# Moving loads, two block transpositions and four totals within the heads stage of a two-layer hybrid backbone kernel

## Chip, cores and metric
One core of a Trainium2 chip. The metric is the device time of one execution in microseconds, the median of several runs.

## The reference, cut to what matters
The reference is a two-layer network on 1024 latent and 256 context tokens, width 1024, all in float32. Layer 0 is a bidirectional gated DeltaNet with 4 heads (beside a pooling branch), layer 1 a short convolution; each layer ends in a mixture of 16 experts. The change touches DeltaNet and the modulation only:

```python
gam = jnp.cumsum(log_decay.reshape(b, h, n, c), axis=-1)
diff = gam[..., :, None] - gam[..., None, :]
decay = jnp.where(incl, jnp.exp(jnp.where(incl, diff, 0.0)), 0.0)
kk = jnp.einsum('bhnid,bhnjd->bhnij', k, k)
t_mat = jnp.eye(c) + jnp.where(strict, kk * decay, 0.0) * beta[..., :, None]
u  = solve(t_mat, v * beta[..., None])        # unit lower triangular
wk = solve(t_mat, k * (beta * jnp.exp(gam))[..., None])
...
sh1, sc1, g1, sh2, sc2, g2 = jnp.split(silu(c) @ ada_w[i] + ada_b[i], 6, axis=-1)
```

For each head, direction and chunk a triangular matrix is made from the decays and from k k^T, and inverted. The modulation is a product of one row with a 1024 x 6144 matrix for each layer.

## The kernel before, in words
The program is one long list of steps that a planner puts in order. The planner places, on each engine, what is ready first, and among ready work what was traced first (`urgent` moves steps ahead by an offset). So the trace order is a preference, the data and buffers decide, and each engine, and SP's queue of DMA issues too, then runs its list strictly in order.

The heads stage is the loop over H = 4 heads in `hybrid_dit_kernel` (L1632 to L1648). `weave` (L832) mixes several lists of steps in proportion: step i of a list of n stands at (i + 0.5)/n. In turn h of the loop three weaves follow one another: the last projection span of head h with `front(h, 0)`; the first span of head h + 1 with `front(h, 1)`, the first eight steps of `invert(h - 1)` and the first half of the modulation's steps; the second span of head h + 1 with `front(h, 2)` and `base(h)`, the other eight steps of `invert(h - 1)`, the decays of head h + 1, and the second half of the modulation's steps.

What the lists hold:
- `project` (L1068): matmuls (tile pq, through `mm3`, L140 to L142), six to a product step, and `convolve` on ScalarE and VectorE (L1090, L1091).
- `decays` (L1140): three groups of chunks (4, 4 and 2). A step allocates the tile L (tag L4 with 4 buffers, two heads' worth; tag L2 with 2), loads the rows of decays from memory, broadcast over the partitions (L1149, two DMAs), and subtracts and masks them on VectorE (L1155, 16 operations of 128x128 for the two large groups, 4 for the small). A last step takes the exponential (L1162).
- `front` (L1166): norms, transposes to token order, k k^T and q k^T (pkk), VectorE's products with L (L1223, L1228), stores of the corner blocks (L1236).
- `base` (L1247): loads the 32x32 corner blocks of 40 items in two directions into X and M (L1262), turns the 40 x 1024 block of X into M (L1264, always on VectorE), clears X (L1265, L1266), eliminates 31 columns with two operations each (L1275, L1278; on GpSimd for heads 0 to 2, on VectorE for head 3), turns the 104 x 1024 result (L1282, always on VectorE) and stores it (L1287).
- `invert` (L1301): loads W (L1313) and builds the 128x128 inverses from the blocks with small matmuls (pinv, L1332) in 16 steps: load, then pairs up to `fourth`, then `fifth` and `sixth` for each of three groups. `fifth` reads L for the last time; after it L's buffer is free for the load of the head after next. `sixth` ends in VectorE's copies into Y (L1392, L1393).
- `ada_blocks` (L782): 2048 columns of the modulation's row, in `parts` of 512 columns (4 parts in the heads stage, 1 elsewhere): eight `products` (DMA of `ada_w`, L797, into a ring of three buffers; VectorE adds into the one buffer adsum, L800 and L802), then `total` (a TensorE matmul with ones, L810, into pad).

The four lines that set the counts before:

```python
        steps += [lambda h=h, k=k: products(h, k) for k in range(KD)] + [lambda h=h: total(h)]   # 9 a part
                weave(project(h + 1, 0), front(h, 1), before[:8], ada[h][:18])
                weave(
                    project(h + 1, 1), base[:-3], before[8:] + mx.decays(h + 1, E[h + 1], heads), ada[h][18:],
```

After the loop come the remaining projections (pz), `base(3)` on VectorE, two scans of two heads each (psc; the second needs sets of all inverses, loaded from memory), and the rest of the network.

## Time and profile before

| what | us |
|---|---|
| median of 3 runs | 1884.71 |
| the runs | 1881.73 to 1886.57 |
| the profiled execution | 1886.57 |
| its span, first to last instruction | 1884.9 |
| TensorE busy in the span | 1659.9 (88%) |
| VectorE busy | 1302.0 (69%) |
| ScalarE busy | 899.6 (48%) |
| GpSimd busy | 531.3 (28%) |

The heads stage lies between 136 and 453 us of the span. Engines are PE (TensorE, its weight loads PEld), DVE (VectorE), ACT (ScalarE), POOL (GpSimd) and SP, whose queue issues the DMAs. In a timeline the bracket at the end of a row is the time that the engine stood idle before it, and what ended that. The clock is the mean granted clock of TensorE, 1.00 for 2.4 GHz.

### The profile page before, as it was taken

The page shows a single profiled execution, that of the slowest core. Times are in us where ns is not written, and L with a number is a line of the kernel's source. Part 1 is how long each engine was busy: PE and PEld are TensorE (multiplying, and loading weights), DVE is VectorE, ACT ScalarE, POOL GpSimd, SP SyncE. Part 2 cuts the span into 40 slices and gives each one's busy share as a digit, 9 for nine tenths or more (in the row PEclk, how much of TensorE's full clock was granted, in tenths as well). Part 3 has the DMA queues.
Part 4 walks back from the last instruction along what each step waited for, and adds up shares of the span by engine and source line. Part 5 has one row for each costly group of instructions (what it writes and reads, how often), then busy time and mean ns, then how long its engine had stood idle before and what let it go on. Part 6 is the DMA issues. An engine that isn't in the chain of part 4 may idle for free.

```text
span 1884.9 us, 26146 instructions
## 1 busy us (share of the span) xinstructions
PE 1659.9 (88%) x9593; PEld 1332.0 (71%) x9593; DVE 1302.0 (69%) x1978; ACT 899.6 (48%) x1586; POOL 531.3 (28%) x551
## 2 busy tenths in 40 slices
PE   6999998789979881999999989999999559989995
PEld 2998875667867661777777777888887347767773
DVE  4628785657778876778888768343444658788897
ACT  3635332523742353777766452101133358778673
POOL 4310286471331154112121261000022512112222
PEclk7989998879999985999999999999999769999998
DMA  7417665649576965799999657422264449999995
GB/s 285 148 35 228 216 200 132 160 151 283 165 291 205 380 223 209 251 350 347 373 360 358 195 181 261 169 95 83 95 226 155 172 137 320 373 338 364 371 334 196
DMA packets 261399, 443.72 MB, mean 235 GB/s; under 512 B 46522, under 2 KB 108715, under 8 KB 257175
## 3 DMA queue, kind: packets, MB, share of 16 engines
q1 hardware_dynamic: 252198, 408.76, 62.7%
q0 software_dynamic: 9072, 33.30, 7.0%
q8 instruction: 75, 1.23, 0.3%
q14 instruction: 54, 0.43, 0.1%
HBM read 368.65 MB, written 73.35 MB: 234 GB/s over the span
## 4 chain that ended last, share of the span: by engine, by line
PE 49%; DVE 14%; DMA 7%; ACT 5%; issue 5%; SPq 2%; POOL 1%; DVEq 0%; ACTq 0%; POOLq 0%
PE py L466 5%; PE gu L141 5%; PE gu L142 4%; PE gu L140 4%; PE pin L140 4%; PE pin L141 4%; PE pin L142 4%; DVE wlo L89 3%; PE po L140 3%; PE po L141 3%; PE po L142 3%; ACT whi L88 2%; PE py L469 1%; DVE junk L315 1%; ACT oh L367 1%
## 5 line engine op out<-in xcount | busy, mean ns | idle before, releaser
L89 DVE TENSOR_TENSOR wlo<-raw,whi 128x2048 fp32r<-128x2048 f32 (+3 forms) x245 | 471.4, 1956 | 79.1 <-ACT whi L88 79.0
L88 ACT CAST whi<-raw 128x2048 fp32r<-128x2048 f32 (+3 forms) x271 | 420.7, 1597 | 219.7 <-PE pin L141 77.7
L141 PE MATMUL gu<-wlo,xh 128*128 128x512 f32 x512 | 209.4, 410 | 11.4 <-DVE wlo L89 11.4
L140 PE MATMUL gu<-whi,xh 128*128 128x512 f32 x512 | 206.7, 408 | 7.7 <-ACT whi L88 6.2
L142 PE MATMUL gu<-whi,xl 128*128 128x512 f32 x512 | 205.3, 404 | 0.4 <-DVE xl L135 0.4
L476 POOL DMA_INDIRECT acc<-y,idx x31 | 80.7, 2603 | 363.7 <-DVE y L471 346.2
L141 PE MATMUL pin<-h1T,whi 128*128 128x512 f32 x384 | 149.9, 392 | 0.0
L142 PE MATMUL pin<-h1T,wlo 128*128 128x512 f32 x384 | 149.4, 391 | 0.0
L140 PE MATMUL pin<-h1T,whi 128*128 128x512 f32 x384 | 148.6, 396 | 0.0
L89 POOL TENSOR_TENSOR wlo<-raw,whi 128x1024 fp32r<-128x1024 f32 (+2 forms) x26 | 80.5, 3117 | 177.4 <-ACT whi L88 166.8
L141 PEld LDWEIGHTS gu<-wlo,xh 128*128 128x128 f32 x512 | 99.0, 193 | 37.2 <-DVE wlo L89 14.9
L140 PEld LDWEIGHTS gu<-whi,xh 128*128 128x128 f32 x512 | 98.8, 193 | 33.4 <-ACT whi L88 8.5
L142 PEld LDWEIGHTS gu<-whi,xl 128*128 128x128 f32 x512 | 98.6, 193 | 22.9 <-DVE xl L135 0.9
L466 PE MATMUL py<-whi,hh 128*128 128x512 f32 x256 | 104.2, 410 | 8.5 <-ACT hh L134 8.4
L802 DVE SCALAR_TENSOR_TENSOR adsum<-raw,cs,adsum 128x512 f32<-128x512 f32 (+1 forms) x77 | 94.9, 1233 | 21.8 <-DMA raw<-in_ada_w_dram 21.2
L466 PE MATMUL py<-wlo,hh 128*128 128x512 f32 x256 | 103.7, 406 | 0.1
L373 POOL DMA_INDIRECT xg<-table,idx x32 | 51.2, 1600 | 176.3 <-ACT idx L371 137.1
L140 PE MATMUL pq<-hT,whi 128*128 128x512 f32 (+1 forms) x256 | 99.0, 387 | 2.1 <-DVE cv L1090 2.0
L367 ACT ACTIVATE oh<-places,aff 128x128 f16<-128x128 f16 x256 | 77.9, 394 | 45.3 <-DVE aff L356 45.3
L141 PE MATMUL pq<-hT,whi 128*128 128x512 f32 (+1 forms) x256 | 98.4, 385 | 0.0
L142 PE MATMUL pq<-hT,wlo 128*128 128x512 f32 (+1 forms) x256 | 98.2, 384 | 0.0
L141 PE MATMUL po<-wlo,mh 128*128 128x512 f32 x224 | 91.6, 409 | 4.9 <-DVE wlo L89 4.9
(393 smaller groups left out, 3733.9 us busy)
## 6 DMA issues: line engine op xcount, KB each, us to landing
raw<-in_w_gate_dram SPq DMA_DIRECT2D x64, 1024.0 KB
raw<-in_w_up_dram SPq DMA_DIRECT2D x64, 1024.0 KB
raw<-in_w_down_dram SPq DMA_DIRECT2D x64, 1024.0 KB
raw<-in_ada_w_dram SPq DMA_DIRECT2D x32, 1024.0 KB
raw<-in_ada_w_dram SPq DMA_DIRECT2D x64, 256.0 KB
raw<-in_sc_w_in_dram SPq DMA_DIRECT2D x12, 1024.0 KB
table<-h SPq DMA_DIRECT2D x16, 520.0 KB
raw<-in_ev_w_in_dram SPq DMA_DIRECT2D x16, 512.0 KB
```

The costliest lines, as they stand in the source:

```text
L88: nc.scalar.copy(hi[:, part], raw[:, part])
L89: (lo_engine or e).tensor_sub(lo[:, part], raw[:, part], hi[:, part])
L140: nc.tensor.matmul(out, lhs[0], rhs[0], start=start, stop=False)
L141: nc.tensor.matmul(out, lhs[0], rhs[1], start=False, stop=False)
L142: nc.tensor.matmul(out, lhs[1], rhs[0], start=False, stop=stop)
L315: nc.vector.tensor_scalar(junk, self.v, cand.bitcast(F32), 0.0, op0=ALU.is_ge, op1=ALU.add, accum_out=cnt)
L367: nc.scalar.activation(oh[:, t, :], co.places, AF.Sign, bias=self.before[:, t, e : e + 1])
L373: nc.gpsimd.indirect_dma_start(out=xg, out_offset=None, in_=self.table[:, :], in_offset=bass.IndirectOffsetOnAxis(ap=idx, axis=0))
L466: nc.tensor.matmul(py, hh[:, k, :], g[w][:, k, :], start=k == w == 0, stop=False)
L469: nc.tensor.matmul(py, hl[:, k, :], g[0][:, k, :], start=False, stop=k == 3)
L476: self.scattered = nc.gpsimd.indirect_dma_start(out=self.acc[:, :], out_offset=bass.IndirectOffsetOnAxis(ap=idx, axis=0), in_=y, in_offset ...
L802: nc.vector.scalar_tensor_tensor(st["sum"], raw, cs[:, k, 0:1], st["sum"], op0=ALU.mult, op1=ALU.add)
```

## The change
Three edits, in the heads stage only.
1. `ada_blocks` with more than one part puts an empty step ahead of each `total` and one behind it: 11 steps a part where there were 9, 45 with the end where there were 37. The first weave of a turn takes 22 of them (two parts, as before) and the second the rest.
2. `decays` gives two lists: three `load` steps (tile and DMAs) and the `prepare` steps with the exponential. In turn 0, which has no inversion, the loads stand ahead of the preparation. In the others the list of the second weave is: fourth, fourth, fifth, sixth, fifth, sixth, load, fifth, load, sixth, load, then three preparations and the exponential: 15 steps where there were 12.
3. The two turning copies in `base` run on the engine of the columns: GpSimd for heads 0 to 2, VectorE as before for head 3.

```diff
@@ ada_blocks
     for h in range(parts):
-        steps += [lambda h=h, k=k: products(h, k) for k in range(KD)] + [lambda h=h: total(h)]
+
+        gap = [lambda: None] if parts > 1 else []
+        steps += [lambda h=h, k=k: products(h, k) for k in range(KD)] + gap + [lambda h=h: total(h)] + gap
     return steps + [end]
@@ Mixer0.decays
-        def prepare(c0, n):
+        def load(c0, n):
             e = pool.tile([P, 2, n, P], F32, tag=f"L{n}", name=co.name("L"), bufs=4 if n == 4 else 2)
             E.append(e)
             for d in range(2):
...
+
+        def prepare(g):
+            e, (c0, n) = E[g], GROUPS[g]
             for d in range(2):
                 for c in range(n):
                     nc.vector.scalar_tensor_tensor(
...
-        return [lambda c0=c0, n=n: prepare(c0, n) for c0, n in GROUPS] + [exp]
+        return [lambda c0=c0, n=n: load(c0, n) for c0, n in GROUPS], [lambda g=g: prepare(g) for g in range(len(GROUPS))] + [exp]
@@ Mixer0.base, begin and end
-            nc.vector.tensor_copy(M[0:40], X[0:40].rearrange("p r c -> p c r"))
+            engine.tensor_copy(M[0:40], X[0:40].rearrange("p r c -> p c r"))
...
-            nc.vector.tensor_copy(XT[:R], X[:R].rearrange("p r c -> p c r"))
+            engine.tensor_copy(XT[:R], X[:R].rearrange("p r c -> p c r"))
@@ hybrid_dit_kernel
-        weave(project(0, 1), mx.decays(0, E[0], heads))
+        loads, rest = mx.decays(0, E[0], heads)
+        weave(project(0, 1), loads + rest)
...
-                weave(project(h + 1, 0), front(h, 1), before[:8], ada[h][:18])
+                weave(project(h + 1, 0), front(h, 1), before[:8], ada[h][:22])
                 ahead = fetch(h + 2)
-                weave(
-                    project(h + 1, 1), base[:-3], before[8:] + mx.decays(h + 1, E[h + 1], heads), ada[h][18:],
-                )
+
+                loads, rest = mx.decays(h + 1, E[h + 1], heads)
+                after = before[8:]
+                if after:
+                    n = len(after)
+                    after = after[: n - 2] + [loads[0], after[n - 2], loads[1], after[n - 1], loads[2]]
+                else:
+                    after = loads
+                weave(project(h + 1, 1), base[:-3], after + rest, ada[h][22:])
```

## Rows read from the trace of the kernel before
**Rows 1.** The windows of the heads stage and of the first scan: from and to in us, length, then for PE, PEld, DVE, ACT and POOL the busy us and the number of instructions, then the mean granted clock, the share of the DMA engines and GB/s.
```profile
136.00:265.00 129.00, 125.47 (x657) 101.59 (x657) 98.82 (x229) 50.10 (x101) 43.26 (x55) 1.00 0.69 211
300.00:326.00 26.00, 22.02 (x286) 15.81 (x284) 14.58 (x22) 6.05 (x12) 23.32 (x39) 0.87 0.28 89
326.00:343.00 17.00, 6.34 (x43) 5.52 (x39) 14.67 (x36) 6.81 (x14) 9.20 (x13) 0.65 0.57 177
390.00:414.00 24.00, 15.68 (x79) 12.96 (x77) 16.53 (x51) 7.71 (x18) 18.17 (x26) 0.62 0.53 159
```
**Rows 2.** Who waited for whom, of TensorE alone, 130 to 500 us: us in total, times, longest.
```profile
PE pinv L1332 <- DVE Y L1393: 11.4, 2, 7.0
PE pad L810 <- DVE adsum L802: 7.0, 2, 4.0
```
**Rows 3.** The same of VectorE, 136 to 505 us.
```profile
DVE L L1155 <- DMA L<-d_gT: 21.1, 5, 6.6
DVE base L1264 <- DMA base<-d_blk: 16.2, 4, 6.2
DVE adsum L800 <- PE pad L810: 7.4, 3, 5.9
```
**Rows 4.** The chain that ended last, from 425 us on: start, us, what.
```profile
425.12 0.26 POOL base L1278
...
428.40 5.04 DMA d_inv<-base
...
433.89 1.57 SPq L1313
...
451.58 1.16 PE psc L1429 x8
...
513.37 4.96 DMA sets<-d_A
```
**Rows 5.** Windows of 10 us around three stalls of TensorE, columns as in rows 1.
```profile
260.00:270.00 10.00, 6.94 (x34) 5.54 (x34) 10.00 (x21) 4.21 (x10) 9.06 (x13) 0.83 0.70 184
280.00:290.00 10.00, 8.41 (x36) 6.78 (x34) 4.19 (x11) 1.28 (x3) 3.91 (x7) 0.66 0.62 136
300.00:310.00 10.00, 6.02 (x174) 3.49 (x172) 5.62 (x9) 2.86 (x7) 8.74 (x17) 0.85 0.37 124
310.00:320.00 10.00, 10.00 (x62) 7.91 (x63) 3.65 (x6) 1.52 (x3) 9.13 (x16) 0.80 0.08 28
```
**Rows 6.** Timelines of VectorE and of TensorE around 282 us: start, us, engine, line, operation, what, idle before.
```profile
281.24 1.08 DVE L1282 COPY base<-base 104x1024 f32<-104x1024 f32 x1 [2.15 <-POOL base L1278]
...
283.82 0.79 PE L140 MATMUL pq<-hT,whi 128*128 128x512 f32 x1 [1.59 <-DVE cv L1090]
```
**Rows 7.** Timeline of TensorE: two totals, and two projection matmuls one behind the other at full clock.
```profile
264.68 1.04 PE L810 MATMUL pad<-adsum,ones 128*32 128x512 f32 x2 [3.06 <-DVE adsum L802]
...
299.32 0.39 PE L141 MATMUL pq<-hT,whi 128*128 128x512 f32 x1
299.55 0.40 PE L142 MATMUL pq<-hT,wlo 128*128 128x512 f32 x1
...
308.01 1.92 PE L810 MATMUL pad<-adsum,ones 128*32 128x512 f32 x2 [3.98 <-DVE adsum L802]
```
**Rows 8.** Timelines of VectorE and of SP's queue, 291 to 297 us.
```profile
291.40 0.49 DVE L800 TENSOR_SCALAR adsum<-raw,cs 128x512 f32<-128x512 f32 x1 [5.90 <-PE pad L810]
295.50 1.12 DVE L1264 COPY base<-base 40x1024 f32<-40x1024 f32 x1 [3.62 <-DMA base<-d_blk]
...
286.74 4.26 SPq L1313 DMA_DIRECT2D W<-d_inv  x4
...
293.41 1.43 SPq L797 DMA_DIRECT2D raw<-in_ada_w_dram  x3
```
**Rows 9.** Timelines of SP, TensorE and VectorE around the loads of the decays' rows, and VectorE's turning copy at 425 us.
```profile
143.07 2.91 SPq L1149 DMA_DIRECT2D L<-d_gT  x6
...
317.50 2.88 SPq L1149 DMA_DIRECT2D L<-d_gT  x4
...
316.77 1.15 PE L1332 MATMUL pinv<-W,L 64*64 64x64 f32 x32
...
311.69 1.33 DVE L1375 COPY Y<-W 64x512 f32<-64x512 f32 x2
...
320.68 2.90 DVE L1155 SCALAR_TENSOR_TENSOR L<-L,g_G,maskf 128x128 f32<-128x128 f32 x4 [6.62 <-DMA L<-d_gT]
...
425.53 1.10 DVE L1282 COPY base<-base 104x1024 f32<-104x1024 f32 x1
```
**Rows 10.** Groups by line of 130 to 500 us (busy us, mean ns of one, idle before), and two single column operations of GpSimd from its timeline.
```profile
L1265 POOL MEMSET base<- 128x1024 f32 x4 | 3.8, 956 | 32.0 <-DVE base L1264 22.0 <-DMA d_q<-cv 10.0
L1266 POOL TENSOR_SCALAR_AFFINE_SELECT base<-base 128x1024 f32<-128x1024 f32 x4 | 5.8, 1457 | 0.1
L1264 DVE COPY base<-base 40x1024 f32<-40x1024 f32 x4 | 4.4, 1108 | 16.2 <-DMA base<-d_blk 16.2
L1282 DVE COPY base<-base 104x1024 f32<-104x1024 f32 x4 | 4.3, 1068 | 2.2 <-POOL base L1278 2.2
...
320.49 0.65 POOL L1275 TENSOR_TENSOR base<-base,base 104x255 f32<-104x255 f32 x1
323.51 1.18 POOL L1275 TENSOR_TENSOR base<-base,base 104x255 f32<-104x255 f32 x1
```

## The prediction, made before the changed kernel ran
> **What bounds the kernel now.** First the windows by stage [rows 1]. The change works in the heads stage, 136 to 453 us. Up to 265 us TensorE is busy 125.5 of 129 us at full clock and sets the pace; from 265 to 414 us it loses time, in three of these stretches: busy 22.0 of 26, 6.3 of 17, 15.7 of 24, at a mean granted clock of 0.87, 0.65 and 0.62. So what this stage is worth is read from what TensorE waits for. Its own waits [rows 2] name two things: 11.4 us for the copies into Y (VectorE, L1393) and 7.0 us for the modulation's last product (VectorE, L802) ahead of a total (L810). Both name VectorE, though VectorE is not full there: VectorE's waits [rows 3] show that its queue stands still, 21.1 us for the decays' rows from memory, 16.2 us for the blocks ahead of their transposition (L1264), 7.4 us for a total; ahead of the second transposition (L1282) it waited 2.2 us for GpSimd [rows 10]. The three parts of the change aim at these four waits. What follows the stage starts from it: in the chain that ended last [rows 4] GpSimd's last column of head 2, the turned blocks' store and the load of W stand one behind the other up to the sets of the second scan. I therefore count a microsecond won before 414 us as won at the end, if this chain comes earlier too.
>
> **Each stall of TensorE costs twice.** Where it idles, the granted clock falls to the lower of its two levels (1.2 GHz) for some microseconds after. Slices of 10 us [rows 5]: a mean of 0.66 means that 6.8 us of the slice ran at 1.2 GHz, so 3.4 us are lost beside the idle time itself; 0.83 is 1.7 us lost, 0.85 and 0.80 behind one another are 3.5.
>
> **T1, transposition L1282 off VectorE.** At 281 us, at the end of head 0's base, VectorE waits 2.15 us for GpSimd, turns the blocks in 1.08, and only then does the convolution that TensorE wants: TensorE idles 1.59 us and goes on at the low clock [rows 6]. With the turning on GpSimd this wait has no reason left. 1.59 plus half of the 3.4 us at the low clock (part of the slice lies ahead of this stall's end, so I don't take it all): **3.3 us**, bounds 0 and 5.0. The same copy for heads 1 and 2 has no stall of TensorE right behind it: nothing more.
>
> **T2 and T3, totals a step later, and L1264 off VectorE.** TensorE stood twice at a total: 3.06 us at 262 and 3.98 at 304 us [rows 7]. A step put ahead of them is about one product step of the woven projection, six matmuls at 0.23 us from one start to the next [rows 7], 1.4 us: TensorE has that much to do while the last product ends. T3 (the stall at 262): 1.4 of 3.06 plus half of 1.7 of clock: **2.2**, bounds 0 and 4.8. T2 (the stall at 304): VectorE also comes earlier, by the copy L1264 itself, 1.1 us; its 3.62 us wait ahead of that [rows 8] I don't count, because the next data of the modulation were issued on SP's queue only at 293.41, behind the loads of W [rows 8]. So 1.1 and 1.4 of 3.98, plus half of 3.5: **4.2**, bounds 0 and 7.5. The step behind a total gives VectorE as much again before it overwrites the sum; the single buffer of the sum stays.
>
> **T4, loads of the decays' rows as steps.** The load is late because the buffers are: for head 2 it is issued at 317.50, 0.7 us after the matmuls that read the old tiles began at 316.77, on an SP queue that had nothing else [rows 9]. A step of its own cannot go ahead of those reads. What changes is that the weave has 15 steps where it had 12, so the third of them, the reading one, stands at 2.5/15 and not 2.5/12 of a stretch of 26 us (300 to 326 [rows 1]): 1.1 us earlier for the rows of heads 2 and 3 alike, **2.2 us**. Bounds: 0, and 11.4, the whole of TensorE's wait for Y, which stands behind VectorE's 6.62 us wait for the rows and the 16 operations on them [rows 9]. Head 1's rows were loaded from 143.07 on [rows 9], long before they are read, and cost nothing either way. The loads of each head are six issues on SP as before, and the queue stood at this wait before as well, so its wait costs nothing new.
>
> **T5, the last head.** It still uses VectorE for its columns, and L1282 of head 2 stands among the first of them (425.53, 1.10 us [rows 9]); gone from there the columns end earlier: **1.1 us**, bounds 0 and 1.1.
>
> **T6, what GpSimd pays.** No row shows such a copy on GpSimd. Bounds by the nearest rows [rows 10]: below, the memset of 128x1024, 0.96 us; a pass with one input over as much, affine_select, 1.46; above, the column operation, 0.65 us for 255 elements, so 2.6 for 1024, and 1.18 for 255 beside VectorE's work, so 4.7. The column operations read across the rows in steps, as the turning does, so I take 2.6, against 1.07 to 1.11 on VectorE [rows 10]: 1.5 us more. In heads 0 and 1 both copies are covered: GpSimd waited 22.0 us for L1264 in any case [rows 10], and between its last column and the next head's first copy it has nothing to do. In head 2 both lie on the chain of [rows 4]: **minus 3.0**, bounds plus 0.2 and minus 7.2. The Trainium skill (GPSIMD Engine Reference, Engine selection) says that passes with one input run at roughly VectorE's rate there: by that T6 would be 0 and the sum 10.3. Its section on performance pitfalls charges 2.9 cycles an element for reads in steps of over 8 bytes, here 128: an estimate of 2.5 us at its 1.2 GHz, and a sum of 7.5. No run here shows either.
>
> **What is late next.** T1 and T2 give TensorE 7.5 us by 317 us, but the reading matmuls at 316.77 also want Y's copies, which VectorE ended at 311.69 plus 1.33 [rows 9]: TensorE can come 3.7 us earlier, VectorE itself 1.1 more. I take 4.8 of the 7.5 and take off **2.7**.
>
> **Sum:** 3.3 + 2.2 + 4.2 + 2.2 + 1.1 - 3.0 - 2.7 = 7.3 us. The profiled execution took 1886.57 us (span 1884.9), 1.86 above the median of the runs, 1884.71. Against its own time that is 1879.3; against the median **1877.4 us**. A measurement of this kernel can tell about 0.3%, 5.7 us, from no change.
>
> **Rivals.**
> A, the wait for the rows goes too: earlier reads and lower priority of the 16 operations let Y's copies go first on VectorE. For it: they are separate steps now, and the loads and the operations had one place. Against: VectorE takes what is ready, and the operations were ready. 11.4 in place of T4's 2.2: 1868.2. 12%.
> B, VectorE's row of waits from 300 to 343 us takes back what TensorE wins: T1, T2 and T4 are lost in it, 2.2 + 1.1 - 3.0 = 0.3 is left: 1884.4. For it: VectorE does 14.7 of 17 us there with TensorE at 6.3 [rows 1]. 20%.
> C, slower: the totals come too late for VectorE. The sum has one buffer, so the next part's first product waits for the total; at 291.40 it had waited 5.90 us because TensorE had a row of matmuls ahead of the total [rows 8]. Put a step later, each of the 8 totals stands another 1.4 us behind; if VectorE gets to the next part before the second step has passed, that is 8 x 1.4 = 11.2 us of standing queue, and T2 and T3 are gone: 1884.71 - (3.3 + 2.2 + 1.1 - 3.0) + 11.2 = 1892.3. It decides where these waits, 7.4 us now, pass 15. Against: the step behind the total moves the product as well. 20%.
> D, the order on the engines stays what it was, since ready work goes first whatever step it was in, and the copies on GpSimd are covered: 1884.7. 6%.
> The forecast has 42%, with a range of its own from 1872 to 1882.
>
> **How the numbers follow.** Range 1866 to 1893: from A with a little of T4's clock up to C. Faster by over 0.3%, below 1879.1: A and 34 of the forecast's 42, 0.46. Within: the other 8, B and D, 0.34. Slower: C, 0.20.
>
> **What would show it.** T1: no wait of TensorE for a convolution at about 283 us, clock above 0.9 in that slice. T2 and T3: TensorE's wait for the modulation under 2 us in all (7.0 now). T4: VectorE's wait for the decays' rows still above 12 us, with the load still right behind the reading matmuls. T5: the last head's columns begin under 1 us after head 2's last column and run without a turning copy. T6: a turning copy on GpSimd of 2 to 3.3 us. I am wrong if the copy takes over 5 us, if VectorE's wait for totals grows, or if the first scan begins no earlier than at 451.58 us [rows 4].

## The result, and the profile after

| | before | changed |
|---|---|---|
| median | 1884.26 us (4 runs) | 1904.28 us (4 runs) |
| lowest to highest | 1881.73 to 1886.57 | 1898.26 to 1907.00 |
| ratio, 95% interval | | 1.0111, 1.0087 to 1.0135 |
| span of the profiled execution | 1884.9 | 1905.3 |
| TensorE busy in it | 1659.9 | 1658.0 |

The changed kernel is 20 us slower; the prediction was 7 us faster, with 1893 as its upper end. TensorE does the same work in the same busy time, so the 20 us are waits, and not in the stage that was edited. In the heads stage the waits that the change aims at fell, but for two, and the last projection came earlier. TensorE isn't busier everywhere there: in the two windows from 300 to 343 us it is busy 27.2 us, 28.4 before. The windows that answer to [rows 1]:

```profile
136.00:265.00 129.00, 127.74 (x677) 103.11 (x675) 106.93 (x246) 52.46 (x104) 47.62 (x60) 1.00 0.75 232
300.00:326.00 26.00, 15.07 (x274) 11.84 (x274) 15.17 (x24) 6.95 (x12) 21.89 (x36) 0.85 0.21 62
326.00:343.00 17.00, 12.12 (x57) 10.20 (x56) 9.78 (x32) 5.75 (x13) 11.34 (x17) 0.53 0.50 163
390.00:414.00 24.00, 16.21 (x78) 13.36 (x75) 12.04 (x46) 8.60 (x21) 16.95 (x26) 0.57 0.64 185
```

The waits of TensorE in the changed kernel, 130 to 500 us [rows 2], and those of VectorE, 136 to 505 us [rows 3]:

```profile
PE pinv L1337 <- DVE Y L1398: 15.2, 2, 10.4
PE pad L810 <- DVE adsum L802: 1.8, 1, 1.8
```

```profile
DVE W L1371 <- ACT W L1373: 25.1, 4, 11.0
DVE L L1160 <- DMA L<-d_gT: 21.0, 5, 6.0
DVE base L1269 <- DMA base<-d_blk: 6.1, 1, 6.1
DVE adsum L800 <- PE pad L810: 0.7, 1, 0.7
```

TensorE's wait at the totals fell from 7.0 to 1.8 us, VectorE's for a total from 7.4 to 0.7, its wait ahead of the first turning copy from 16.2 to 6.1 (for heads 0 to 2 it is GpSimd that waits now, 10.5 us). The wait for the decays' rows stayed, TensorE's wait for Y grew, and VectorE's largest wait is a new one, 25.1 us for ScalarE's W, 6.7 before. (Lines behind L828 are two to five further down than before: L1282 is L1287, L1313 is L1318, L1332 is L1337.) TensorE's last projection matmul (pz) started at 442.1 us, 449.2 before.

The turning copies on GpSimd, which no row of before could show [rows 10] (busy us, mean ns of one, idle before):

```profile
L1287 POOL COPY base<-base 104x1024 f32<-104x1024 f32 x3 | 6.2, 2060 | 0.2
L1269 POOL COPY base<-base 40x1024 f32<-40x1024 f32 x3 | 6.0, 2001 | 10.6 <-DMA base<-d_blk 10.5
```

Then it turns. Windows of 10 us from 440 us on, first the kernel before, then the changed one (columns as in rows 1; the second number is TensorE's busy time, the third number from the end its clock):

```profile
440.00:450.00 10.00, 9.22 (x264) 6.99 (x265) 5.68 (x15) 2.60 (x6) 0.00 (x0) 1.00 0.91 287
450.00:460.00 10.00, 9.10 (x119) 7.86 (x120) 9.56 (x33) 4.95 (x15) 2.23 (x1) 1.00 0.91 287
460.00:470.00 10.00, 9.24 (x77) 8.67 (x76) 6.68 (x21) 6.39 (x26) 1.79 (x4) 1.00 1.02 370
470.00:480.00 10.00, 8.30 (x71) 7.91 (x71) 4.54 (x13) 6.78 (x29) 3.56 (x8) 1.00 0.77 180
```

```profile
440.00:450.00 10.00, 5.09 (x97) 3.79 (x96) 1.58 (x5) 1.52 (x4) 0.00 (x0) 0.89 1.09 265
450.00:460.00 10.00, 8.45 (x229) 7.12 (x228) 6.85 (x22) 4.90 (x13) 0.00 (x0) 0.77 1.05 375
460.00:470.00 10.00, 8.92 (x78) 8.01 (x78) 8.21 (x27) 3.63 (x13) 2.23 (x1) 0.83 0.84 301
470.00:480.00 10.00, 6.93 (x107) 6.45 (x108) 2.31 (x7) 2.59 (x12) 1.78 (x4) 0.66 0.47 73
```

TensorE is through with its projections 7 us earlier and has little to do: 5.09 us busy where it was 9.22. ScalarE shows most of the reason. It runs its list in order, and the last projection's z stands in it ahead of the inverse's step B (L1351, L1346 before), where B came first before. Its rows, first of the kernel before, then of the changed one, and TensorE's first product of the scan in the changed one:

```profile
442.09 0.44 ACT L1346 ACTIVATE B<-pinv 128x320 f32<-128x320 f32 x1 [0.16 <-PE pinv L1332]
450.93 0.60 ACT L1131 ACTIVATE z<-pz 128x512 f32<-128x512 f32 x1 [1.33 <-DMA d_z<-z]
```

```profile
447.87 0.60 ACT L1133 ACTIVATE z<-pz 128x512 f32<-128x512 f32 x1 [10.64 <-DMA d_z<-z]
448.36 0.43 ACT L1351 ACTIVATE B<-pinv 128x320 f32<-128x320 f32 x1
448.51 2.07 PE L1434 MATMUL psc<-hT 128*128 128x128 f32 x8 [3.84 <-ACT z L1133]
```

The z waits 10.64 us for its buffer, which the store of an earlier z must free; B waits behind it and comes at 448.36 (442.09 before), and the scan's first product waits 3.84 us.

From here on no step was edited, and the two programs differ in the order in which they were built. Three marks tell the rest: the first gate-and-up matmul (gu) of the first expert stage, 755.1 before and 764.8 changed; the first expert stage, from there to the short convolution's first matmul, 343.0 and 344.9 us; the second, from its first gate-and-up matmul to the last down matmul, 317.6 and 325.0 us. So 7 us won by 442, 17 lost up to the experts, 9 lost in the experts, some more in between. Of the 17, 4 are lost between the last projection and the first scan's first product (6.4 us, 2.4 before), 11.7 in the first scan (71.3 us from its first product to its last, 59.6 before), and 1 behind it.

**First difference, the scans.** In TensorE's list head 3's first inverse products (pinv) stand after 87 of the first scan's 176 products before, and after 36 changed. TensorE reaches them with 36 done, and W isn't there (timeline of the changed kernel):

```profile
469.38 0.39 PE L1444 MATMUL psc<-w,hT 128*128 128x128 f32 x2
473.07 0.28 PE L1337 MATMUL pinv<-W,L 32*32 32x32 f32 x2 [3.31 <-DMA W<-d_inv]
```

It waits 3.31 us with the scan's steps behind it and goes on at a clock of 0.66 in that slice, then runs head 3's inverse with a scan that is 38 products back: at 479.05 us, where the kernel before began this inverse with 87 done, it has 49. The built list carries this on: the out-projection's first product stands after 107 of the second scan's products, 144 before. TensorE, VectorE and GpSimd of the changed kernel there:

```profile
556.64 0.79 PE L140 MATMUL po<-whi,mh 128*128 128x512 f32 x1 [7.20 <-ACT whi L88]
560.68 1.22 PE L1434 MATMUL psc<-r,sets 128*128 128x128 f32 x4 [3.25 <-DVE r L1431]
565.87 0.79 PE L141 MATMUL po<-wlo,mh 128*128 128x512 f32 x1 [3.97 <-DVE wlo L89]
```

```profile
555.67 4.69 DVE L135 TENSOR_TENSOR ml<-mt,mh 128x512 fp32r<-128x512 f32 x1 [6.96 <-ACT mh L134]
560.81 10.50 DVE L89 TENSOR_TENSOR wlo<-raw,whi 128x1024 fp32r<-128x1024 f32 x2
571.94 0.68 DVE L135 TENSOR_TENSOR ml<-mt,mh 128x512 fp32r<-128x512 f32 x1
```

```profile
550.85 19.38 POOL L96 TENSOR_TENSOR raw<-raw,bc 128x2048 f32<-128x2048 f32 x4 [24.06 <-DMA zs<-d_z]
```

14.4 us of waits in the 18 from 549 to 567 (6.1 in the same stretch before), with 69 of the second scan's products still to come. VectorE's operation took 4.69 us beside GpSimd's and 0.68 after it. The Trainium skill (SBUF — State Buffer, SBUF: two separate sides) says that a GpSimd operation that reads SBUF and a VectorE one with two SBUF inputs lock each other out for a whole instruction; this trace agrees. But the kernel before has the same pair, so it is not what the change added:

```profile
548.31 18.39 POOL L96 TENSOR_TENSOR raw<-raw,bc 128x2048 f32<-128x2048 f32 x4 [30.48 <-PE psc L1439]
557.50 4.83 DVE L135 TENSOR_TENSOR ml<-mt,mh 128x512 fp32r<-128x512 f32 x1
```

**Second difference, the experts.** No edit touches them, yet TensorE's order in them is another one. Their windows in the changed kernel (those of the kernel before stand with the run "no edit, cut at 20" below):

```profile
764.80:1109.80 345.00, 319.49 (x1490) 250.23 (x1490) 279.26 (x222) 236.71 (x285) 66.76 (x40) 0.97 0.93 317
1550.80:1875.80 325.00, 307.17 (x1440) 243.91 (x1440) 260.61 (x187) 226.62 (x270) 67.43 (x29) 0.96 0.93 314
```

In the second TensorE has the same 1440 matmuls and is busy 4 us longer, at a mean clock of 0.96 for 0.98.

### The profile page after: what moved, and what is told of

Read it like the earlier page. It is cut to its first block, busy times and chain, and to the rows that moved or that the text cites. A ratio compares the mean times of both kernels' runs of the same rounds, so it can differ in the third digit from the quotient of the medians.

```text
span 1905.3 us, 26107 instructions
## 1 busy us (share of the span) xinstructions
PE 1658.0 (87%) x9593; PEld 1332.1 (70%) x9593; DVE 1295.0 (68%) x1972; ACT 899.9 (47%) x1586; POOL 537.4 (28%) x557
## 4 chain that ended last, share of the span: by engine, by line
PE 39%; DVE 10%; issue 8%; DMA 8%; ACT 4%; POOL 1%; DVEq 0%; SPq 0%; POOLq 0%; ACTq 0%
PE pin L140 4%; PE pin L142 4%; PE pin L141 4%; DMA acc<-y,idx 4%; PE py L466 3%; PE gu L140 3%; PE gu L141 3%; PE gu L142 3%; PE po L142 3%; PE po L141 3%; PE po L140 3%; DVE wlo L89 3%; ACT whi L88 2%; DMA xg<-table,idx 1%; DVE junk L315 1%
## 5 line engine op out<-in xcount | busy, mean ns | idle before, releaser
L89 DVE TENSOR_TENSOR wlo<-raw,whi 128x2048 fp32r<-128x2048 f32 (+3 forms) x245 | 480.8, 1996 | 69.5 <-ACT whi L88 69.2
L140 PE MATMUL po<-whi,mh 128*128 128x512 f32 x224 | 93.3, 417 | 7.2 <-ACT whi L88 7.2
L140 PE MATMUL pq<-hT,whi 128*128 128x512 f32 (+1 forms) x256 | 96.9, 379 | 0.0
L141 PE MATMUL pq<-hT,whi 128*128 128x512 f32 (+1 forms) x256 | 96.3, 376 | 0.0
```

The lines of the kernel that those rows point to most:

```text
L89: (lo_engine or e).tensor_sub(lo[:, part], raw[:, part], hi[:, part])
L140: nc.tensor.matmul(out, lhs[0], rhs[0], start=start, stop=False)
L141: nc.tensor.matmul(out, lhs[0], rhs[1], start=False, stop=False)
```

## The experiments

"Place" below is how many of the first scan's 176 products TensorE started ahead of head 3's first inverse product; experts' order is that of TensorE's matmuls, by name, in the two stages ("but 2": two matmuls of one stage stand elsewhere). The diffs are cut to the lines that matter; where the first weave of a turn takes another number of the modulation's steps, the second takes the rest. Times of stages are of one profiled execution; ratios are to the kernel before, measured beside each. The letters H, O, G and so on are the theories that the expectations name.

| kernel | place | experts' order | first gu, us | experts, us | ratio, 95% interval |
|---|---|---|---|---|---|
| before | 87 | before | 755.1 | 343.0 + 317.6 | |
| before again | 87 | before | 750.1 | 342.6 + 318.4 | |
| loads | 87 | before | 750.1 | 340.5 + 318.9 | 0.9993, 0.9978 to 1.0009 |
| one copy (head 2) | 78 | before, but 2 | 754.6 | 340.3 + 318.4 | 1.0005, 0.9984 to 1.0025 |
| gaps 21 and loads | 87 | before | 745.7 | 342.0 + 317.7 | 0.9998, 0.9982 to 1.0014 |
| whole, both orders mended | 77 | before | 752.0 | 340.4 + 315.3 | 1.0010, 0.9993 to 1.0027 |
| gaps | 78 | second | 754.9 | 348.0 + 327.1 | 1.0061, 1.0041 to 1.0080 |
| gaps and loads | 78 | second | 749.6 | 348.9 + 325.3 | 1.0075, 1.0053 to 1.0096 |
| no edit, cut at 20 | 78 | second | 753.3 | 347.0 + 328.0 | 1.0067, 1.0048 to 1.0086 |
| turns | 33 | before, but 2 | 766.3 | 340.6 + 319.3 | 1.0069, 1.0041 to 1.0097 |
| whole, cut at 21 | 33 | before, but 2 | 773.0 | 340.3 + 314.6 | 1.0068, 1.0043 to 1.0092 |
| no edit, inverse early | 30 | own | 765.1 | 342.9 + 319.8 | 1.0105, 1.0077 to 1.0133 |
| changed | 36 | third | 764.8 | 344.9 + 325.0 | 1.0111, 1.0087 to 1.0135 |
| changed again | 36 | third | 756.5 | 347.1 + 321.2 | |
| whole, scan mended | 79 | third | 755.8 | 344.1 + 323.6 | 1.0077, 1.0050 to 1.0104 |
| whole, edge | 79 | own | 754.4 | 339.3 + 321.8 | 1.0078, 1.0050 to 1.0106 |
| turns, edge | 81 | third, but 2 | 752.2 | 339.5 + 325.5 | 1.0084, 1.0058 to 1.0109 |

**Gaps alone**, the first edit:

```diff
+        gap = [lambda: None] if parts > 1 else []
+        steps += [products ...] + gap + [total] + gap
-                weave(project(h + 1, 0), front(h, 1), before[:8], ada[h][:18])
+                weave(project(h + 1, 0), front(h, 1), before[:8], ada[h][:22])
```

> The kernel before with the first edit alone: the modulation's totals one step later, two empty steps a part, 22 steps in a head's first projection. Theory H (hand-off): the change wins some 7 us until the last z projection (start of its last matmul 449.2 before, 442.1 after) and loses them and more behind it, because GpSimd's turning copy splits the stores of head 2's inverse, SyncE puts the scan's loads between them, and head 2's rows come to TensorE 2.6 us later (all 74 first products 441.2 before, 443.8 after) though its elimination ended 3.8 us earlier. By H this kernel, which has no copy on GpSimd, keeps what the totals give: last z projection at 444 to 447, time 1878 to 1883. Rival O (order): every edit rearranges the whole program's order on all engines, in stages that it does not touch too (the second expert stage took 7 us more after); by O the time may stand anywhere from 1876 to 1900 and its stages differ with no link to the edit. Rival G: it is the totals that do the harm; then 1895 to 1905.

1894.68 us, slower by 0.6%, against 1878 to 1883 by theory H. Up to the experts it is level with the kernel before (754.9); it loses 5.0 and 9.5 us in the two expert stages.

**Loads alone**, the second edit:

```diff
+        return [load ...], [prepare ...] + [exp]
+                after = after[: n - 2] + [loads[0], after[n - 2], loads[1], after[n - 1], loads[2]]
```

> The kernel before with the second edit alone: the loads of the decays' rows as steps of their own. VectorE's wait for those rows was over 12 us in heads 2 and 3, and the loads come 1 to 3 us earlier. Theory H: last z projection within 2 us of 449.2, time 1881 to 1886 (no change). Rival O: anywhere from 1876 to 1900. Rival L, the loads delay something else on SyncE's queue: 1887 or more, with the last z projection later than 450.

1881.28 us, no difference that shows (0.9978 to 1.0009 leaves room for the 2.2 us of T4).

**Turns alone**, the third edit:

```diff
-            nc.vector.tensor_copy(M[0:40], X[0:40] ...)
+            engine.tensor_copy(M[0:40], X[0:40] ...)
-            nc.vector.tensor_copy(XT[:R], X[:R] ...)
+            engine.tensor_copy(XT[:R], X[:R] ...)
```

> The kernel before with the third edit alone: both turning copies of heads 0 to 2 on GpSimd (1.9 to 2.1 us each in the changed kernel, 1.07 to 1.11 on VectorE before). Theory H: the elimination of heads 0 to 2 ends some 2 us later per head, the stores of head 2's inverse are split in SyncE's queue as in the changed kernel, and the first products of head 2 come late; last z projection at 446 to 450, then a wait of 3 us or more before the scan; time 1888 to 1900. Rival O: anywhere from 1876 to 1900, and the stores of head 2's inverse need not be split. Rival V: VectorE is the engine that gains, 1878 to 1883.

1896.02 us, slower by 0.7%, and all of it lies ahead of the experts (766.3). The number was H's; its reason fell with a later run.

**Gaps and loads**, the change without its third edit:

```diff
+        steps += [products ...] + gap + [total] + gap
+                after = after[: n - 2] + [loads[0], after[n - 2], loads[1], after[n - 1], loads[2]]
```

> The changed kernel without its third edit: totals a step later and loads as steps, turning copies on VectorE. Theory H: the hand-off to the scans is not spoiled, time 1876 to 1883, faster than before. Rival O: anywhere from 1876 to 1900, no sum of the two single edits. Rival G, the totals do the harm: 1895 to 1905.

1897.84 us: like gaps alone, and the experts' order is the same, matmul for matmul. H fell for the gaps; G and O were left.

**No edit, cut at 20**: the kernel before, with nothing but this:

```diff
-                weave(project(h + 1, 0), front(h, 1), before[:8], ada[h][:18])
+                weave(project(h + 1, 0), front(h, 1), before[:8], ada[h][:20])
-                ... ada[h][18:],
+                ... ada[h][20:],
```

> The kernel before with no edit of its own work: only the number of modulation steps in a head's first projection is 20 and not 18, so that two products of the second part come some us earlier. The four kernels so far fall into two groups: the kernel before, loads alone and turns alone have the very same order of TensorE's matmuls in the first expert stage (first gate-and-up matmul to the short convolution's first: 343.0, 340.5, 340.6 us) and took 317.6 to 319.3 us in the second; gaps alone and gaps with loads share another order and took 348.0, 348.9 and 327.1, 325.3 us. This kernel has the order of the second group, without one empty step. Theory O (the order of the expert stages, which no edit touches, costs the gaps their time): first expert stage 346 to 350 us, second 324 to 328, time 1892 to 1899. Rival G (the gaps' own late totals do it): stages as before, 341 to 344 and 317 to 320, time 1881 to 1887.

1897.65 us, slower by 0.67%. Two products of the modulation put into the earlier of two weaves cost 4 us in the first and 10 in the second expert stage. Windows over the two expert stages, of the kernel before again and then of this one:

```profile
750.10:1092.80 342.70, 320.62 (x1490) 253.55 (x1490) 281.60 (x222) 236.25 (x285) 66.45 (x40) 0.96 0.94 319
1532.50:1850.90 318.40, 303.00 (x1440) 240.56 (x1440) 260.39 (x187) 227.53 (x270) 71.72 (x29) 0.98 0.94 320
```

```profile
753.30:1100.30 347.00, 321.06 (x1490) 252.91 (x1490) 279.17 (x222) 237.20 (x285) 66.78 (x40) 0.96 0.92 315
1541.80:1869.80 328.00, 308.00 (x1440) 245.38 (x1440) 260.74 (x187) 227.86 (x270) 60.87 (x29) 0.96 0.91 311
```

The same 1490 and 1440 matmuls; in the second stage TensorE waits 4.6 us more and is busy 5 us longer at a lower clock. The rate of memory is lower too, 311 GB/s for 320, but over 328.0 us and 318.4 that is the same number of bytes. Its waits there, 1530 to 1871 us, again first the kernel before again:

```profile
PE py L466 <- ACT hh L134: 7.4, 5, 2.7
PE gu L140 <- ACT whi L88: 1.6, 2, 0.9
```

```profile
PE gu L140 <- ACT whi L88: 8.4, 4, 3.5
PE py L466 <- ACT hh L134: 2.9, 3, 1.8
```

In the other order it waits for freshly split weights (whi), 8.4 us for 1.6, and less for hh, 2.9 for 7.4. So O holds: the gaps' price is that of an order they did not aim at.

**Gaps 21 and loads**: as gaps and loads, with a cut that gives the experts the order of before.

```diff
-                weave(project(h + 1, 0), front(h, 1), before[:8], ada[h][:22])
+                weave(project(h + 1, 0), front(h, 1), before[:8], ada[h][:21])
```

> Gaps and loads without the turning copies, with 21 modulation steps in the first projection in place of 22: the expert stages then have the order of the kernel before. Theory O: what gaps and loads gave up to the first gate-and-up matmul (5.5 us at 22 steps) stays to the end: that matmul at 748 to 752, expert stages 341 to 344 and 317 to 320 us, time 1876 to 1881, faster than before. Rival G: 1893 to 1899 as with 22 steps. Rival N (the gain ahead of the experts is given back there whatever the order): 1882 to 1886.

1884.06 us, ratio 0.9998: the 12 us of gaps and loads are gone with one step, as O said. But it is not faster than before either; rival N had the number. (The profile is of one of its fastest executions, 1876.92 us, so the 745.7 of the table is early for it.)

**One copy**, head 2's second turning copy alone on GpSimd:

```diff
+            (nc.gpsimd if h == 2 else nc.vector).tensor_copy(XT[:R], X[:R] ...)
```

> The kernel before with one copy moved: the second turning copy of head 2 alone on GpSimd (2.1 us there, 1.0 on VectorE); all other turning copies stay on VectorE. Theory H (hand-off): in SyncE's order the second pair of stores of head 2's inverse again stands behind loads of the scan (the kernel before has the four stores together), the second pair goes out 5 us or more after the copy's end, head 2's first products come 2 to 8 us later than in the kernel before, and the first gate-and-up matmul starts 7 to 12 us later: time 1891 to 1897, nearly all of what the three heads' copies cost together (1896.0). Rival S (the copies' own longer time in all heads, 1 us each on the path): about a sixth of it, 1884 to 1887. Rival F (the first copies of the heads do it): 1882 to 1886.

1883.59 us. In SP's queue the stores did go apart and W did come late: the second pair of stores at 433.52, 4.8 us behind the copy's end, W's loads at 438.73 (433.52 before), head 2's first products at 442.6 (437.9 and 433.5 in the two executions of before). The first gate-and-up matmul didn't move. So theory H, late rows of head 2, is wrong: other work of TensorE covers them.

**Whole, cut at 21**: the same cut in the changed kernel, which gives the first expert stage the order of before, and the second that of turns alone.

```diff
-                weave(project(h + 1, 0), front(h, 1), before[:8], ada[h][:22])
+                weave(project(h + 1, 0), front(h, 1), before[:8], ada[h][:21])
```

> The whole change with 21 modulation steps in the first projection in place of 22: TensorE's order in the first expert stage is then that of the kernel before, and in the second that of turns alone. If H and O are the two halves of the loss, this keeps H and drops O: first gate-and-up matmul 763 to 768 as in the changed kernel (764.8), expert stages 340 to 343 and 317 to 320 us, time 1892 to 1897. Rival G: 1902 to 1907, as with 22 steps.

1898.10 us, ratio 1.0068: what the experts cost is gone (340.3 and 314.6 us), what the scans cost stays (773.0, more than expected). Place 33, as with turns alone.

**Whole, edge**: the changed kernel, and head 3's first products held behind the fifth pass of the scan.

```diff
+            inverse = urgent(invert(H - 1))
+            def held():
+                with tc.issue_after(mx.done[4]):   # the pass's last K matmul on TensorE
+                    inverse[1]()
-            weave(steps[:n], urgent(invert(H - 1)))
-            weave(steps[n:])
+            weave(steps[:20], inverse[:1])
+            weave(steps[20:20 + n], [held] + inverse[2:])
+            weave(steps[20 + n:])
```

> The whole change, with one order edge more: on TensorE the first products of head 3's inverse stand behind the fifth pass of the first scan. In TensorE's order they then come after 79 of that scan's 176 products, as they come after 87 in the kernel before and after 36 in the changed kernel; the out-projection's first product comes after 140 of the second scan's products (144 before, 107 changed). Nothing else is changed by hand, but the order of the expert stages becomes one that no kernel so far had. Theory I (the place of head 3's inverse in TensorE's order is what the turning copies cost): first gate-and-up matmul 749 to 757 in the profiled execution (764.8 changed, 755.1 before), no wait of TensorE for the rows W of head 3 over 2 us, time 1885 to 1898 by what the experts' order costs. Rival P (the slower copies themselves, or the head's late rows): that matmul at 762 to 768, time 1898 to 1907.

First gate-and-up matmul 754.4, within I's range, P's was 762 to 768. TensorE has no wait where W's products stand:

```profile
479.61 0.47 PE L1442 MATMUL psc<-wd,hT 128*128 128x128 f32 x2
480.00 0.89 PE L1337 MATMUL pinv<-W,L 32*32 32x32 f32 x80
```

The median, 1892.09, stays 0.8% above before. The profiled execution (1887.8) was this kernel's fastest; what the slower ones lost isn't located.

**Turns, edge**: the same edge on turns alone.

```diff
+                with tc.issue_after(mx.done[4]):
+                    inverse[1]()
```

> The kernel before with the turning copies on GpSimd, and the same order edge: head 3's first products after 81 of the scan's 176 products (33 without the edge, time 1896.0). Theory I: first gate-and-up matmul 751 to 758 (766.3 without the edge), time 1880 to 1893 by the experts' order, which is a new one here too. Rival P: 763 to 769, time 1893 to 1900.

First gate-and-up matmul 752.2, 766.3 without the edge, as I said. 1894.23 us is a little over its range: the second expert stage, in the changed kernel's order matmul for matmul, took 325.5 us (325.0 there). The first, in that order but for two matmuls, took 339.5, where the changed kernel's took 344.9 and 347.1; so the order of TensorE's list is not all that sets the first stage's time.

**No edit, inverse early**: the kernel before with an edge the other way, no copy moved.

```diff
+            weave(steps[:10], inverse[:2])
+            def held():
+                with tc.issue_after(mx.product):   # head 3's first products on TensorE
+                    steps[10]()
+            weave([held] + steps[11:10+n], inverse[2:])
```

> The kernel before with no copy moved, but with one order edge the other way: a step of the first scan stands behind head 3's first products, which so come after 30 of the scan's 176 products (87 in the kernel before), and the out-projection's first product after 98 of the second scan's. Theory I: the loss of the turning copies comes without them: TensorE waits 3 us or more for the rows W of head 3, the first scan ends 8 to 16 us later than in the kernel before (its last product 511.2), first gate-and-up matmul 764 to 775, time 1892 to 1906. Rival P: the scan's products fill in behind, that matmul at 752 to 758, time 1880 to 1889.

```profile
460.36 0.39 PE L1439 MATMUL psc<-w,hT 128*128 128x128 f32 x2
474.28 0.28 PE L1332 MATMUL pinv<-W,L 32*32 32x32 f32 x2 [13.53 <-DMA W<-d_inv]
```

The loss of the turning copies comes without them: first gate-and-up matmul 765.1, last product of the first scan 525.9 (511.2 before), 1900.95 us.

**Before again**, for scatter.

> The kernel before once more, unchanged, for a second profile: how far a stage's time differs between two executions of one program. All theories: time 1875 to 1890; last z projection, first gate-and-up matmul and the expert stages within 5 us of 449.2, 755.1, 343.0 and 317.6 us. If the last z projection or the first gate-and-up matmul comes more than 4 us earlier, the gains of gaps and loads there (5 to 9 us) are scatter.

Last z projection 444.8, first gate-and-up matmul 750.1: 4.4 and 5.0 us ahead of the first execution of the very same program, the expert stages within 0.8. So gains of 5 us in the heads of one profile are scatter.

**Whole, both orders mended**: the changed kernel with its edge behind the nineteenth step of the scan, which leaves the experts the order of before.

```diff
+                with tc.issue_after(mx.done[18]):   # counted by steps here
+                    inverse[1]()
+            weave(steps[:19], inverse[:1])
+            weave(steps[19:19 + n], [held] + inverse[2:])
```

> The whole change, all three edits at 22 steps, and one order edge on TensorE: head 3's first products behind the nineteenth step of the first scan. They then come after 77 of its 176 products (36 changed, 87 before), and TensorE's order in the expert stages and in the short convolution is matmul for matmul that of the kernel before. Theory I with O (the two orders are the whole loss): first gate-and-up matmul 746 to 757, expert stages 340 to 345 and 316 to 320 us, time 1876 to 1887, no slower than before; if the heads had also kept what the prediction said, 1874 to 1880. Rival R (a rest of the loss lies in the edits' own work): 1889 or more.

1881.67 us, ratio 1.0010 (0.9993 to 1.0027), 1.0% under the changed kernel's. All three edits are in it, with GpSimd's copies. So one order edge takes the loss back; to 0.3% the edits as a whole cost nothing, and they win nothing. TensorE is nearly as idle behind the projections as in the changed kernel:

```profile
440.00:450.00 10.00, 5.64 (x99) 4.03 (x98) 3.56 (x9) 0.85 (x2) 0.00 (x0) 0.98 1.15 240
```

**Whole, scan mended**: the changed kernel with a cut at 18 and the edge behind the fifth pass; the experts' order is the changed kernel's.

```diff
-                weave(project(h + 1, 0), front(h, 1), before[:8], ada[h][:22])
+                weave(project(h + 1, 0), front(h, 1), before[:8], ada[h][:18])
+                with tc.issue_after(mx.done[4]):
+                    inverse[1]()
```

> The whole change with 18 steps and an order edge that holds head 3's first products behind the fifth pass of the first scan, 79 of 176; TensorE's order in the expert stages is matmul for matmul that of the changed kernel. Theory I with O: first gate-and-up matmul 746 to 757, but the expert stages 344 to 348 and 323 to 327 us as in the changed kernel (345.0 and 325.0), time 1889 to 1897, some 10 us more than the kernel with the experts' order of before. Rival R, or the experts' stage times are scatter: 1878 to 1887.

1895.26 us, 13.6 more than the last; experts 344.1 and 323.6. Each number is as O and I had it, but the first gate-and-up matmul's with the help of early heads: the last z projection came at 436.9, and from there it took 318.9 us, as long as in the two profiles of the changed kernel (322.7 and 318.6).

**Changed again.**

> The changed kernel once more, for a second profile. All theories: time 1897 to 1908. By I and O the first gate-and-up matmul within 5 us of 764.8 and the expert stages within 2 us of 345.0 and 325.0; the last z projection tells how much the heads really gained: over 4 us ahead of the kernel before's second profile (444.8) the prediction's heads were right, under 3 us they were not.

1897.63 us. Last z projection 437.9: the mean of two executions is 440.0, of before 447.0, so the heads did come about 7 us earlier, with 4 us between executions. Its first gate-and-up matmul is 8 us ahead of the first profile's, and its expert stages miss what was expected (within 2 us of 345.0 and 325.0) by a little: scatter as wide as the effect, which is why the theory rests on the groups. Place 30 to 36, five profiles: 756.5 to 773.0, mean 765.1. Place 77 to 87, twelve profiles: 745.7 to 755.8, mean 752.3.

## Why the prediction was wrong, step by step

**T1** (3.3 us): the wait for the convolution at 283 us is gone and the slice's clock is 1.00. TensorE is busy no longer in it (8.22 us, 8.41 before), because a wait of 1.78 us at a total stands there now, and the clock of 1.00 held through it: not each stall costs twice, as the prediction took it. And in the second execution of the kernel before the wait was gone as well. The same program, 0 to 100 and 280 to 290 us, in its first execution (the second slice is in [rows 5]) and in its second:

```profile
0.00:100.00 100.00, 80.98 (x546) 65.58 (x547) 54.86 (x115) 46.47 (x98) 34.63 (x74) 0.87 0.59 204
```

```profile
0.00:100.00 100.00, 79.98 (x554) 65.28 (x554) 55.20 (x117) 47.80 (x101) 34.76 (x74) 0.92 0.59 205
280.00:290.00 10.00, 9.27 (x52) 6.70 (x53) 1.73 (x7) 1.71 (x4) 2.94 (x3) 1.00 0.90 160
```

The clock in that slice was 0.66 in one and 1.00 in the other. T1 was worked out from a stall that the program has in one of these two executions only.

**T2, T3** (6.4): right in kind. The waits at the totals were 7.0 and 7.5 us in the two executions of before, 1.8 and 2.4 in those of the changed kernel.

**T4** (2.2): VectorE's wait for the rows stayed, 21.0 us. The rest can't be told: with loads alone the reading matmuls began at 310.84 us, in the two executions of before at 316.77 and 311.97.

**T5** (1.1): head 3's columns begin on VectorE at 421.65, head 2's last on GpSimd at 421.36; the turning copy no longer stands among them. But the 1.1 us were not won: VectorE's second operation stood beside GpSimd's copy and took 1.97 us, 0.21 before, so that the third began 2.24 us behind the first, 1.39 before (425.40 to 426.79).

```profile
421.65 0.21 DVE L1280 TENSOR_TENSOR base<-base,base 104x31 f32<-104x31 f32 x1 [3.87 <-POOL base L1283]
421.89 1.97 DVE L1283 TENSOR_TENSOR base<-base,base 104x31 f32<-104x31 f32 x1
421.68 2.10 POOL L1287 COPY base<-base 104x1024 f32<-104x1024 f32 x1
```

**T6** (minus 3.0): the copies take 2.00 and 2.06 us, not 2.6, so the two cost 1.9. The second sets off more in SP's queue, which the prediction didn't count: the stores of the inverse stand there in two pairs with the scan's loads between them, and W's loads go out at 435.77 us, 433.52 before, although GpSimd's last column came 3.8 us earlier. With one copy moved this costs nothing that shows at the end (1.0005). The rule of the Trainium skill that the prediction set beside it (GPSIMD Engine Reference, Engine selection), VectorE's rate, doesn't hold for this copy: VectorE takes 1.07 to 1.11 us [rows 10]. The estimate by the same page's section on performance pitfalls, 2.5, was nearer.

**Late next** (minus 2.7): TensorE's wait for Y grew by 3.8 us, from 11.4 to 15.2.

**The sum**, up to the end of the projections, came out: 7.0 us by two executions each, 7.3 predicted. With T1 worked out from a stall of one execution, T4 not to be told and T5 not won, that is luck in part; the four other builds with all three edits had their last z projection between 436.9 and 447.6 us.

What failed is the sentence ahead of the terms, "I therefore count a microsecond won before 414 us as won at the end, if this chain comes earlier too", in two ways. The gain isn't passed on: where both orders were mended the time is that of before (1.0010), as it is for gaps 21 and loads (0.9998). That is the value of rivals B and D, 1884. The chain's condition wasn't met either: its column came earlier, its loads of W later (T6). Where the gain goes shows in the stretch from the last z projection to the first gate-and-up matmul: 305.6 us in the mean of eight profiles that have neither the three heads' copies on GpSimd nor an early inverse, 313.3 in the four with these copies and an edge that holds the inverse, 321.5 in the five with an early inverse. Those four end their projections 5.8 us earlier than the eight by the means (440.3 for 446.1) and give it back there. All eight profiles with the three heads' copies have 5.4 to 6.7 us between the last projection and the scan, the nine others 2.4 to 4.4, and in seven of the eight ScalarE's last z waits 9.6 to 10.9 us for its buffer, 1.3 in both executions of before. No run moves this wait alone, so how much of the gain it takes is open.

The other way costs most of the 20 us: the prediction took the order of everything behind the heads as given. The planner's list is one piece, and edits rearranged it. Turns moved head 3's inverse 54 products ahead in the first scan (33 for 87): 13 us by the means of the two groups. Gaps gave the experts another order: the two stages together took 674 to 675 us in its three profiles, 655 to 661 in the eight with the order of before, or that but for two matmuls. The changed kernel has a loss of each kind; by the means of its two profiles the first gate-and-up matmul is at 760.7, 8 us behind the late-place group, and the experts took 669.1, 10 us more than the mean of those eight, 658.7: 18 of the 20 us. Rival D even named the order, only as a reason for no change. Rival C had the sign with the wrong mechanism: VectorE's waits for totals fell.

The test that the prediction set itself, that the first scan begin before 451.58 us, passed: 448.51. But 4 of the 7 us were gone by then, and the stage whose start it looked at lost 11.7 more.

Not settled is why the planner moved head 3's inverse and the experts: its reasons leave no row in a trace. Shown is that an early inverse without the copies costs what it costs with them (no edit, inverse early), that the gaps' order of the experts without the gaps costs the same (no edit, cut at 20), and that the edits without those orders cost nothing in all. The changed kernel's own order of the experts, the third, was not built without edits; with the turns alone its second stage took as long (325.5), its first, but for two matmuls, didn't (339.5).

## What to carry to other kernels

Where a planner orders the whole program, an edit is two changes: its own work, and a new order for all that comes after it. Compare the built orders engine by engine first; where a stage that the edit doesn't touch has changed, its time is the edit's too, and a change that does nothing (here: two steps moved) tells how much such an order is worth. A term that rests on one stall and the clock behind it wants a second profile of the same program.

## What the runs showed of the hardware

A copy that turns blocks (104x1024, reads 128 bytes apart) took 2.06 us on GpSimd and 1.07 on VectorE. Beside one of 2.10 us on GpSimd a VectorE operation of 104x31 with two inputs took 1.97 us, 0.21 just ahead of it. Two executions of one program differed by 6.1 us at 293 us of the span (first inverse products at 293.1 and 287.0), with a granted clock of 0.87 and 0.92 in the first 100 us.
